# Half of an output projection as seven block products: layer 0's out-projection of a two-layer fp32 trunk on one Trainium2 core

## The chip, the cores and the metric

The kernel runs on one core of one Trainium2 chip. The metric is the device time of one execution in microseconds (us). Engines: PE is TensorE's matmul, PEld its weight load, DVE is VectorE, ACT is ScalarE, POOL is GpSimd, SP is SyncE, which here only issues transfers. An engine executes its instructions in the order in which they stand in the program, and waits on semaphores for what it needs.

## The reference

A causal trunk of two layers on a sequence of 512 tokens with model width 1024, everything in float32. Layer 0 is the one that matters here:

```python
xn = rms_norm(h, norm_mix[layer])
proj = jnp.einsum('bsd,de->bse', xn, w_in_even[i])
y_a = short_gated_conv(a_b, a_c, a_v, conv_a[i])        # 512 channels
y_b = multiscale_pool(z_b, w_pool[i], pool_scale[i])    # 512 channels
mix = jnp.concatenate([y_a, y_b], axis=-1)
h = h + jnp.einsum('bse,ed->bsd', mix, w_out_even[i])   # the output projection
hn = rms_norm(h, norm_ffn[layer])
h = h + gated_conv_ffn(hn, w_gate, w_up, conv_w, conv_b, w_down)
```

Then comes layer 1, with a gated mixer of another kind and an FFN of the same kind, and a last norm. The output projection of layer 0 multiplies the mix (512 tokens, 1024 channels: 512 of y_a, 512 of y_b) with a weight of 1024x1024.

## The kernel before, in words

**Number format.** Each operand of a matmul is split into a high part in fp32r and a low part, the rest; a product is three matmuls, high x high, high x low and low x high (`mm3`, L157 to L159). A weight gets its parts in one of two ways. `parts` (L149) copies the high part on ACT (L152) and subtracts on DVE (L153). `summed` (L138) copies the negative weight on ACT (L142), adds the weight onto it by a DMA on POOL's queue (L144), and copies the high part on ACT (L146). Tiles of weights are 128x1024; there are four "raw" slots for weights as they arrive (`fetch`, L130), and six each for high and low parts. A fetch waits until the slot's last reader is done.

**Layout.** The residual `h` lies as eight tiles of 128 channels x 512 tokens, and so does the mix: `mix[0..3]` of y_a, `mix[4..7]` of y_b. PSUM has seven banks for products and one for small things.

**Layer 0's mixer** (`mixer0`) makes groups of four banks: z, ac, av, then four pooled products pm (L527), then ab. The group ab ends with `b_done`, which multiplies the bank into a tile `cv` and splits it into high and low part.

**The output projection** (`project`, L303, called from `mixer0`, "oe" in the profile) has two halves of 512 output channels, `gi` = 0 and 1. A half is 4 column blocks x 8 k x 3 matmuls of 128x512, 96 in all. The first four k go through all four banks, the other four k ("tail") bank by bank, so that the banks end one after the other. For each one `done` adds the bank to `h[k]` on DVE (L315), and `norm.add` makes the scaled copy for the next product: ACT's high part hg (L202), DVE's low part (L203), ACT's square (L209, L212) and POOL's sum of squares (L213).

**The FFN of layer 0** (`Ffn`) comes next. Its first two channel tiles (f = 0) are a direct product of 512-column matmuls ("gu", `direct`, L645). Its weights come by `pair_weights` (L631, transfers L640). During gu the kernel makes sums of activation blocks (`block_sums`, L675 to L700; the first two of the four sets are split by adding DMAs on POOL, the others on ACT and DVE, L731 and L732), the norm's reciprocal root (`rstd_cols`, L246 to L256), and the weight sums of the next unit (`prepare`, L734 to L777). All later pairs of channel tiles are Strassen units (`products`, L785): seven products of 256-token blocks with 128-column weight blocks, by the helper `multiply` (L558 to L588), which lets products add up in the same half bank:

```python
BANK = {1: "a", 6: "a", 7: "a", 4: "a", 5: "e", 3: "e", 2: "b"}
```

What is in a bank is read out between products: by ACT's copy (L816) or by an add on DVE (L804). A product that goes on in a bank waits for that reader. In the unit f = 2 each product is 12 matmuls of 128x256; from f = 4 on high and low part of the moving block go together as one matmul of 512 columns (L571) and the low weights as one of 256.

**What sets the order.** The code is written without synchronisation: a scheduler lays the instructions of each engine in an order and inserts the waits, and the pools give out the slots. So an edit at one place can change the order of instructions on an engine some way beyond it. `tc.keep_in_program_order` and `behind` pin a few places by hand, none in the output projection.

Of the kernel before, what the change touches and what calls it, by code (L numbers as in the profile page):

```python
# [8 lines left out]
F32 = mybir.dt.float32  # L9
F32R = mybir.dt.float32r  # L10
BF16 = mybir.dt.bfloat16
AF = mybir.ActivationFunctionType
ALU = mybir.AluOpType
PSUM = bass.MemoryType.PSUM

P = 128
D = 1024
S = 512
# [13 lines left out]
def tile_trunk(ctx: ExitStack, tc: tile.TileContext, x, norm_mix, norm_ffn, final_norm,  # L32
# [3 lines left out]
    nc = tc.nc  # L36
    x = x[0]
# [92 lines left out]
    def fetch(src, a, b, name):  # L130
        raw = wp.tile([P, a, b], F32, tag="raw", bufs=4, name=f"raw_{name}")
        nc.sync.dma_start(raw, src)
        return raw, a, b, name
# [27 lines left out]
    def group(name, outs, ks, lhs, rhs, tail, on_done, before=None, at_end=None, begun=None):  # L161

        start, banks = begun or (0, {})
        head = max(0, len(ks) - tail)
        order = [(i, j) for i in range(start, head) for j in outs]
        order += [(i, j) for j in outs for i in range(head, len(ks))]
        at = start - 1  # L170
        for i, j in order:
            if i > at and before is not None:
                before(ks[i])
            at = max(at, i)
            if j not in banks:
                banks[j] = mm_bank(f"{name}_{j}")
            mm3(banks[j], lhs(ks[i], j), rhs(ks[i], j), i == 0, i == len(ks) - 1)
            if i == len(ks) - 1 and at_end is None:
                on_done(j, banks[j])
        if at_end is not None:  # L180
            at_end()
            for j in outs:
                on_done(j, banks[j])


    h = [cp.tile([P, S], F32, tag=f"h{k}", name=f"h{k}") for k in range(NK)]
    hg2 = [cp.tile([P, 2, S], F32R, name=f"hg{k}") for k in range(NK)]
    hg = [(t[:, 0], t[:, 1]) for t in hg2]

    def hg_k(k):  # L190
        return hg[k][0], hg[k][1]
# [71 lines left out]
    def split(pool, src, name, scale=1.0, tag="a", bufs=None):  # L263
        hi = pool.tile([P, S], F32R, tag=f"{tag}hi", bufs=bufs, name=f"{name}_hi")
        lo = pool.tile([P, S], F32R, tag=f"{tag}lo", bufs=bufs, name=f"{name}_lo")
        nc.scalar.activation(hi, src, AF.Copy, scale=scale)
        if isinstance(scale, float):
            nc.vector.tensor_tensor(lo, src, hi.bitcast(F32), ALU.subtract)
        else:
            nc.vector.scalar_tensor_tensor(lo, src, scale, hi.bitcast(F32),  # L270
                                           op0=ALU.mult, op1=ALU.subtract)
        return hi, lo
# [19 lines left out]
    def half_weights(name, w, ks, gi):  # L292

        chunks = {}
        for i in range(0, len(ks), 2):
            k0 = min(ks[i], ks[i + 1])
            hi, lo = weights(
                w[k0 * P : (k0 + 2) * P, gi * 512 : gi * 512 + 512]
                .rearrange("(k p) c -> p k c", p=P), 2, 512, f"{name}_{gi}_{k0}")
            chunks[k0], chunks[k0 + 1] = (hi, lo, 0), (hi, lo, 1)  # L300
        return chunks

    def project(name, w, acts, ks, norm, before=None, halves=(0, 1), tail=4):  # L303

        for gi in halves:
            chunks = half_weights(name, w, ks, gi)

            def lhs(k, j):
                hi, lo, n = chunks[k]
                cs = slice(j * P, (j + 1) * P)  # L310
                return hi[:, n, cs], lo[:, n, cs]

            def done(j, ps):
                k = gi * 4 + j
                nc.vector.tensor_tensor(h[k], ps, h[k], ALU.add)  # L315
                if norm is not None:
                    norm.add(k)

            group(f"{name}{gi}", range(4), ks, lhs, lambda k, j: acts[k], tail, done,
                  before if gi == 0 else None)  # L320


    prm0 = prm1 = None
# [5 lines left out]
    def in_parts(chunks, k, raw, after=(None, None)):  # L329
        hi, lo = parts(*raw, after=after)  # L330
        for i in range(raw[1]):
            chunks[k + i] = hi[:, i, :], lo[:, i, :]

    def in_group(name, w, c0, lhs_is_weight, on_done, tail, chunks=None, before=None,
                 after=(None, None), begun=None, after_later=None):
        if chunks is None:
            chunks = {}
            for k in range(0, NK, 2):
                in_parts(chunks, k, in_fetch(name, w, c0, k, 2),
                         after_later if k and after_later else after)  # L340

        def wt(k, j):
            cs = slice(j * P, (j + 1) * P)
            return chunks[k][0][:, cs], chunks[k][1][:, cs]

        def wt_wide(k, j):
            return chunks[k]

        def tokens(k, j):
            cs = slice(j * P, (j + 1) * P)  # L350
            return hg[k][0][:, cs], hg[k][1][:, cs]

        if lhs_is_weight:
            group(name, range(4), list(range(NK)), wt, lambda k, j: hg_k(k), tail, on_done, before,
                  begun=begun)
        else:
            group(name, range(4), list(range(NK)), tokens, wt_wide, tail, on_done, before)

    def mixer0():
        nonlocal prm0  # L360
        w = w_in_even[0]
        with tc.tile_pool(name="m0", bufs=1) as mp:
# [4 lines left out]
            norm = Norm("m0", lambda k: prm_mix["col"]("mix", k))  # L367
# [81 lines left out]
            mix = {}  # L449
# [3 lines left out]
            zs = {}  # L453
# [36 lines left out]
            prm0 = params0()  # L490
# [21 lines left out]
            cv = {}  # L512

            def v_done(j, ps):
                p = padded_tile()
                nc.vector.tensor_tensor(p[:, 2:], ps, ac[j], ALU.mult)
                if j % 2 == 0:
                    cv["pair"] = mp.tile([P, 2, S], F32, tag="four", bufs=5, name=f"cv{j}")
                t = cv["pair"][:, j % 2, :]
                conv3(t, p, *(prm0("ca", 4 * i + j) for i in range(3)))  # L520
                nc.gpsimd.tensor_tensor(t, t, rstd[0], ALU.mult)
                cv[j] = t

            in_group("av", w, 1024, True, v_done, 4)

            for g in range(4):
                ps = mm_bank(f"pm{g}")  # L527
                mm3(ps, (wpl_hi[:, g, :], wpl_lo[:, g, :]), pooled[g], True, True)
                mix[4 + g] = split(mp, ps, f"yb{g}", scale=prm0("psc", g), tag="mix", bufs=8)

            def b_done(j, ps):
                nc.vector.tensor_tensor(cv[j], ps, cv[j], ALU.mult)
# [2 lines left out]
            in_group("ab", w, 0, True, b_done, 4)  # L535

            nxt = Norm("f0", lambda k: prm0("ffn", k))
            project("oe", w_out_even[0], mix, [4, 5, 6, 7, 0, 1, 2, 3], nxt)
            return nxt

    STEPS = [(0, None, True), (2, (0, 2, 0), False), (4, (0, 2, 1), True)]
    for f in range(6, NF, 4):
        STEPS += [(f, (f - 4, f, 0), False), (f + 2, (f - 4, f, 1), f + 4 < NF)]
    HALF = S // 2
    NP = NK // 2
# [8 lines left out]
    def multiply(banks, name, product, left, right, both=None):  # L558

        at = BANK[product]
        first = at not in banks
        if first:
            banks[at] = mm_bank(f"{name}{at}")
        ps = banks[at][:, :HALF]
        if both is not None:
            for kp in range(NP):  # L570
                nc.tensor.matmul(banks[at], left(kp)[0], both(kp), start=first and kp == 0,  # L571
                                 stop=kp == NP - 1, skip_group_check=True)
            for kp in range(NP):
                last_matmul[0] = nc.tensor.matmul(ps, left(kp)[1], right(kp)[0], start=False,
                                                  stop=kp == NP - 1, skip_group_check=True)
            return banks[at]
        for kp in range(NP):
            (a_hi, a_lo), (b_hi, b_lo) = left(kp), right(kp)
            for l, r, end in ((a_hi, b_hi, False), (a_hi, b_lo, False),
                              (a_lo, b_hi, kp == NP - 1)):  # L580
                nc.tensor.matmul(ps, l, r, start=first, stop=end, skip_group_check=True)  # L581
                first = False
        return ps
# [8 lines left out]
    class Ffn:  # L592
# [109 lines left out]
        def moving(self, product, kp):  # L702

            if product in (1, 2, 3):
                k = kp if product == 1 else kp + NP
                c = slice(HALF, S) if product == 3 else slice(0, HALF)
                return hg[k][0][:, c], hg[k][1][:, c]
            if product in (6, 7):
                t = self.t23[kp][product - 6]
                return t[:, 0, :], t[:, 1, :]  # L710
            return tuple(t[:, {4: 0, 5: 1}[product], :] for t in self.t41[kp])
# [701 lines left out]
    n = mixer0()  # L1413
    n = ffn0(n)
    n = mixer1(n)
# [31 lines left out]
```

## Time and profile before

| | |
|---|---|
| median of 3 runs | 972.64 us (972.55 to 972.85) |
| the profiled execution | 972.66 us |
| its span in the trace | 970.9 us |
| granted PE clock, mean | 0.998 |
| first half of the output projection on PE | 100.62 to 122.38 us |
| its second half | 122.38 to 144.14 us |
| gu, the direct FFN unit | 144.14 to 167.32 us |
| f = 2, the first Strassen unit | 167.32 to 187.50 us |

Times in the trace count from the span's start. A line of the timeline gives start, duration, engine, source line and operation, then output <- inputs by the program's names with numbers left out (so `g_2a` is bank "a" of the gate in unit f = 2, and `wlo_g` any low part of a gate's weight), shape and, in brackets, how long the engine had been idle before and what released it. Line numbers are those of the kernel before; in the changed kernel the code behind `mixer0` stands 88 lines lower. Matmuls are pipelined, so their durations overlap and the distance between starts tells what one costs.

### The profile page before, as it was taken

The page shows a single profiled execution, that of the slowest core. Times are in us where ns is not written, and L with a number is a line of the kernel's source. Part 1 is how long each engine was busy: PE and PEld are TensorE (multiplying, and loading weights), DVE is VectorE, ACT ScalarE, POOL GpSimd, SP SyncE. Part 2 cuts the span into 40 slices and gives each one's busy share as a digit, 9 for nine tenths or more (in the row PEclk, how much of TensorE's full clock was granted, in tenths as well). Part 3 has the DMA queues.
Part 4 walks back from the last instruction along what each step waited for, and adds up shares of the span by engine and source line. Part 5 has one row for each costly group of instructions (what it writes and reads, how often), then busy time and mean ns, then how long its engine had stood idle before and what let it go on. Part 6 is the DMA issues. An engine that isn't in the chain of part 4 may idle for free.

```text
span 970.9 us, 13658 instructions
## 1 busy us (share of the span) xinstructions
PE 961.0 (99%) x4952; PEld 818.6 (84%) x4952; DVE 812.9 (84%) x1387; ACT 597.5 (62%) x895; POOL 152.0 (16%) x173
## 2 busy tenths in 40 slices
PE   9999999999999999999999999999999999999996
PEld 7888888988888888888888888889888888888885
DVE  6887458999898998998878675589998989889897
ACT  5523347765675665765586834587665666656775
POOL 3141023110111010110311001221111011100123
PEclk9999999999999999999999999999999999999999
DMA  7442225776777677774352333167767777668775
GB/s 252 149 137 86 87 88 111 178 180 161 195 175 168 157 174 195 168 176 135 128 153 87 109 109 108 51 136 182 185 142 196 195 174 174 159 162 200 195 154 139
DMA packets 92335, 148.33 MB, mean 153 GB/s; under 512 B 5124, under 2 KB 56300, under 8 KB 92268
## 3 DMA queue, kind: packets, MB, share of 16 engines
q1 hardware_dynamic: 76236, 98.69, 32.1%
q0 software_dynamic: 14256, 46.93, 26.8%
q10 hardware_dynamic: 1776, 1.84, 0.6%
q8 instruction: 39, 0.64, 0.3%
q14 instruction: 28, 0.23, 0.1%
HBM read 98.42 MB, written 2.10 MB: 104 GB/s over the span
## 4 chain that ended last, share of the span: by engine, by line
PE 94%; DVE 3%; DMA 1%; issue 1%; ACT 0%; POOLq 0%; DVEq 0%; POOL 0%
PE dn L158 3%; PE dn L159 3%; PE dn L157 3%; PE d L158 3%; PE d L157 3%; PE d L159 3%; PE vu_a L1026 2%; PE gu L157 2%; PE gu L159 2%; PE oo L159 2%; PE oo L157 2%; PE gu L158 2%; PE oe L159 1%; PE oe L158 1%; PE oo L158 1%; PE oe L157 1%
## 5 line engine op out<-in xcount | busy, mean ns | idle before, releaser
L144 POOL DMA_DIRECT2D wlo_g<-raw_g x20 | 17.2, 862 | 318.8 <-ACT wlo_g L142 118.3
L617 DVE SCALAR_TENSOR_TENSOR c<-rows,prm,c 128x512 f32<-128x512 f32 x88 | 65.3, 744 | 1.6 <-ACT c L615 1.4
L158 PE MATMUL dn<-wlo_dn,a_hi 128*128 128x512 f32 x144 | 56.2, 390 | 0.0
L158 PE MATMUL d<-a_lo,whi_d 128*128 128x512 f32 x144 | 56.2, 390 | 0.0
L159 PE MATMUL dn<-whi_dn,a_lo 128*128 128x512 f32 x144 | 56.2, 390 | 0.0
L159 PE MATMUL d<-a_hi,wlo_d 128*128 128x512 f32 x144 | 56.1, 390 | 0.0
L157 PE MATMUL d<-a_hi,whi_d 128*128 128x512 f32 x144 | 56.1, 390 | 0.0
L157 PE MATMUL dn<-whi_dn,a_hi 128*128 128x512 f32 x144 | 56.1, 390 | 0.0
L731 ACT ACTIVATE whi_a<-raw_g 128x512 fp32r<-128x512 f32 x20 | 12.6, 632 | 61.3 <-PE g_10e L571 9.0
L213 POOL TENSOR_TENSOR ssq_f<-ssq_f,sq_f 128x512 f32<-128x512 f32 x14 | 19.8, 1411 | 142.4 <-issue 102.0
L142 ACT ACTIVATE wlo_g<-raw_g 128x1024 fp32r<-128x1024 f32 x20 | 21.2, 1062 | 27.5 <-PE g_2e L581 8.8
L202 ACT ACTIVATE hg<-h,prm 128x512 fp32r<-128x512 f32 x24 | 17.3, 721 | 33.1 <-DVE h L315 33.1
L615 ACT ACTIVATE c<-rows,prm 128x512 f32<-128x512 f32 x44 | 31.4, 715 | 9.8 <-DVE rows L828 9.6
L625 ACT ACTIVATE s<-c,prm 128x512 f32<-128x512 f32 x44 | 31.4, 716 | 6.2 <-DVE c L617 6.1
L1201 DVE SCALAR_TENSOR_TENSOR y<-dn,small,y 128x512 f32<-128x512 f32 x40 | 28.0, 749 | 8.1 <-PE dn L159 8.1
L203 DVE SCALAR_TENSOR_TENSOR hg<-h,prm,hg 128x512 fp32r<-128x512 f32 x24 | 22.6, 944 | 11.9 <-ACT hg L202 11.9
L159 PEld LDWEIGHTS dn<-whi_dn,a_lo 128*128 128x128 f32 x144 | 27.0, 188 | 5.7
L159 PEld LDWEIGHTS d<-a_hi,wlo_d 128*128 128x128 f32 x144 | 27.0, 188 | 5.7
L153 DVE TENSOR_TENSOR wlo_dn<-raw_dn,whi_dn 128x1024 fp32r<-128x1024 f32 x18 | 22.0, 1224 | 11.7 <-ACT whi_dn L152 10.6
L157 PEld LDWEIGHTS d<-a_hi,whi_d 128*128 128x128 f32 x144 | 27.1, 188 | 5.4
L157 PEld LDWEIGHTS dn<-whi_dn,a_hi 128*128 128x128 f32 x144 | 27.1, 188 | 5.4
L158 PEld LDWEIGHTS dn<-wlo_dn,a_hi 128*128 128x128 f32 x144 | 27.0, 188 | 5.4
(1060 smaller groups left out, 3261.6 us busy)
## 6 DMA issues: line engine op xcount, KB each, us to landing
raw_g<-in_w_ffn_gate_dram SPq DMA_DIRECT2D x40, 512.0 KB, 3.8
raw_u<-in_w_ffn_up_dram SPq DMA_DIRECT2D x40, 512.0 KB, 4.3
raw_dn<-in_w_ffn_down_dram SPq DMA_DIRECT2D x22, 512.0 KB, 6.0
wlo_g<-raw_g POOLq DMA_DIRECT2D x20, 512.0 KB, 4.6
wlo_u<-raw_u POOLq DMA_DIRECT2D x20, 512.0 KB, 6.4
raw_d<-in_w_ffn_down_dram SPq DMA_DIRECT2D x18, 512.0 KB, 4.1
wlo_s12g<-s12g POOLq DMA_DIRECT2D x18, 512.0 KB, 6.3
wlo_s34g<-s34g POOLq DMA_DIRECT2D x18, 512.0 KB, 5.7
```

Source lines behind the costliest of these rows:

```text
L142: first = nc.scalar.activation(lo, raw, AF.Copy, scale=-1.0)
L153: behind(nc.vector.tensor_tensor(lo, raw, hi.bitcast(F32), ALU.subtract), after[0])
L157: nc.tensor.matmul(ps, lhs[0], rhs[0], start=start, stop=False)
L158: nc.tensor.matmul(ps, lhs[0], rhs[1], start=False, stop=False)
L159: nc.tensor.matmul(ps, lhs[1], rhs[0], start=False, stop=stop)
L203: nc.vector.scalar_tensor_tensor(hg[k][1], h[k], g, hg[k][0].bitcast(F32), op0=ALU.mult, op1=ALU.subtract)
L213: nc.gpsimd.tensor_tensor(self.ssq, self.ssq, sq, ALU.add)
L615: nc.scalar.activation(c, t[:, 0:S], AF.Copy, scale=prm("cf", ft))
L617: self.last_conv = nc.vector.scalar_tensor_tensor(c, t[:, i : S + i], prm("cf", i * NF + ft), c, op0=ALU.mult, op1=ALU.add)
L625: self.last_silu = nc.scalar.activation(s, c, AF.Silu, bias=self.prm("bf", ft))
L1026: nc.tensor.matmul(banks[at], lhs[l], rhs[r], start=first, stop=end, skip_group_check=True)
L1201: return nc.vector.scalar_tensor_tensor(dst, ps, ffn.cols[:, t : t + 1], dst, op0=ALU.mult, op1=ALU.add)
```

## The change

The second half of the output projection (output channels 512 to 1023) is computed by seven block products (Strassen's scheme in the same variant that the FFN uses) in place of the eight. Tokens are cut into two blocks of 256, the mix into y_a and y_b, and the weight's half into four blocks of 512 x 256. A product is then 4 k x 2 column blocks of 128 x 3 split terms, with 256 columns moving: 24 matmuls of 128x256, and all seven 168.

The block sums of activations are made on DVE during the first half, in place, on the float32 tiles of y_a (`cv`, read through `ya`) and of y_b, of which ACT now makes a float32 copy (`ybr`) beside the split parts. The sums get their own high and low parts: four of 128x512 in `hg4` to `hg7` (free at that time) and eight of 128x256 in slots of the mixer's pool (`t43`). Weight sums are made on DVE in the raw slots; weights of products 1, 2, 4 and 6 are split by `parts`, those of 5, 7 and 3 by `summed`. The order of the products is 1, 2, 6, 5, 7, 3, 4; after each product DVE adds its half bank to a half of `h[k]`, and `norm.add` follows product 3 for `h[4]` and `h[5]` and product 4 for `h[6]` and `h[7]`.

```diff
--- before.py
+++ after.py
@@ -516,17 +516,22 @@
                 nc.vector.tensor_tensor(p[:, 2:], ps, ac[j], ALU.mult)
                 if j % 2 == 0:
                     cv["pair"] = mp.tile([P, 2, S], F32, tag="four", bufs=5, name=f"cv{j}")
+                    ya.append(cv["pair"])
                 t = cv["pair"][:, j % 2, :]
                 conv3(t, p, *(prm0("ca", 4 * i + j) for i in range(3)))
                 nc.gpsimd.tensor_tensor(t, t, rstd[0], ALU.mult)
                 cv[j] = t
 
+            yb, ya = [], []
             in_group("av", w, 1024, True, v_done, 4)
 
             for g in range(4):
                 ps = mm_bank(f"pm{g}")
                 mm3(ps, (wpl_hi[:, g, :], wpl_lo[:, g, :]), pooled[g], True, True)
                 mix[4 + g] = split(mp, ps, f"yb{g}", scale=prm0("psc", g), tag="mix", bufs=8)
+                if g % 2 == 0:
+                    yb.append(mp.tile([P, 2, S], F32, tag="four", bufs=5, name=f"ybr{g}"))
+                nc.scalar.activation(yb[-1][:, g % 2, :], ps, AF.Copy, scale=prm0("psc", g))
 
             def b_done(j, ps):
                 nc.vector.tensor_tensor(cv[j], ps, cv[j], ALU.mult)
@@ -535,12 +540,95 @@
             in_group("ab", w, 0, True, b_done, 4)
 
             nxt = Norm("f0", lambda k: prm0("ffn", k))
-            project("oe", w_out_even[0], mix, [4, 5, 6, 7, 0, 1, 2, 3], nxt)
+            t43 = {}
+
+            def sums_of(k):
+                if k not in (1, 2):
+                    return
+                q = k - 1
+                block_sums_of(ya[q], yb[q])
+                for n in range(2):
+                    kp = 2 * q + n
+                    nc.scalar.activation(hg[4 + kp][0], ya[q][:, n, :], AF.Copy)
+                    nc.vector.tensor_tensor(hg[4 + kp][1], ya[q][:, n, :],
+                                            hg[4 + kp][0].bitcast(F32), ALU.subtract)
+                for i in range(2):
+                    for n in range(2):
+                        at = 4 * q + 2 * i + n
+                        tag, bufs = ("z", 4) if at < 4 else ("zs", 2) if at < 6 else ("pl", 2)
+                        t = mp.tile([P, 2, HALF], F32R, tag=tag, bufs=bufs, name=f"t43_{at}")
+                        src = yb[q][:, n, i * HALF : (i + 1) * HALF]
+                        nc.scalar.activation(t[:, 0], src, AF.Copy)
+                        nc.vector.tensor_tensor(t[:, 1], src, t[:, 0].bitcast(F32), ALU.subtract)
+                        t43[i, 2 * q + n] = t[:, 0], t[:, 1]
+
+            project("oe", w_out_even[0], mix, [4, 5, 6, 7, 0, 1, 2, 3], nxt, before=sums_of,
+                    halves=(0,))
+            project_blocks("oe1", w_out_even[0], mix,
+                           {6: lambda kp: tuple(x[:, :HALF] for x in hg[4 + kp]),
+                            5: lambda kp: tuple(x[:, HALF:] for x in hg[4 + kp]),
+                            4: lambda kp: t43[0, kp], 7: lambda kp: t43[1, kp]}, nxt)
             return nxt
 
 
 
 
+
+    def block_sums_of(y0, y1):
+
+        t3, t1, t2, t4 = y1[:, :, HALF:], y0[:, :, HALF:], y0[:, :, :HALF], y1[:, :, :HALF]
+        nc.vector.tensor_tensor(t3, t3, t1, ALU.subtract)
+        nc.vector.tensor_tensor(t1, t1, t2, ALU.subtract)
+        nc.vector.tensor_tensor(t2, t2, t3, ALU.add)
+        nc.vector.tensor_tensor(t4, t4, t2, ALU.subtract)
+
+    def project_blocks(name, w, acts, sums, norm):
+
+        raw = {}
+        for i, j in ((0, 0), (1, 0), (1, 1), (0, 1)):
+            raw[i, j] = fetch(w[i * 512 : (i + 1) * 512, 512 + j * HALF : 512 + (j + 1) * HALF]
+                              .rearrange("(k p) c -> p k c", p=P), 4, HALF, f"{name}_{i}{j}")
+        stat = {}
+
+        def put(product, how, at):
+            r, a, b, n = raw[at]
+            stat[product] = how(r, a, b, f"{n}_{product}")
+
+        def to(at, x, y, op):
+            nc.vector.tensor_tensor(raw[at][0], raw[x][0], raw[y][0], op)
+
+        a11, a12, a21, a22 = (0, 0), (1, 0), (0, 1), (1, 1)
+        put(1, parts, a11)
+        put(2, parts, a12)
+        put(4, parts, a22)
+        to(a22, a21, a22, ALU.add)
+        to(a21, a11, a21, ALU.subtract)
+        to(a11, a22, a11, ALU.subtract)
+        put(6, parts, a11)
+        to(a12, a12, a11, ALU.subtract)
+        put(5, summed, a22)
+        put(7, summed, a21)
+        put(3, summed, a12)
+
+        def moving(product, kp):
+            if product in (1, 2, 3):
+                c = slice(HALF, S) if product == 3 else slice(0, HALF)
+                return tuple(x[:, c] for x in acts[kp + (0 if product == 1 else NP)])
+            return sums[product](kp)
+
+        banks = ({}, {})
+        for product in (1, 2, 6, 5, 7, 3, 4):
+            for i in range(2):
+                hi, lo = stat[product]
+                c = slice(i * P, (i + 1) * P)
+                ps = multiply(banks[i], f"{name}_{i}", product,
+                              lambda kp: (hi[:, kp, c], lo[:, kp, c]),
+                              lambda kp: moving(product, kp))
+                k = 4 + i + 2 * (product in (5, 7, 4))
+                d = h[k][:, HALF:] if product in (6, 5, 7, 3) else h[k][:, :HALF]
+                nc.vector.tensor_tensor(d, ps, d, ALU.add)
+                if product in (3, 4):
+                    norm.add(k)
 
     STEPS = [(0, None, True), (2, (0, 2, 0), False), (4, (0, 2, 1), True)]
     for f in range(6, NF, 4):
```

## The prediction

> **What bounds the kernel now.** I read the page first, then the waits on PE, then the stages.
>
> ```profile
> span 970.9 us, 13658 instructions
> PE 961.0 (99%) x4952; PEld 818.6 (84%) x4952; DVE 812.9 (84%) x1387; ACT 597.5 (62%) x895; POOL 152.0 (16%) x173
> PE 94%; DVE 3%; DMA 1%; issue 1%; ACT 0%; POOLq 0%; DVEq 0%; POOL 0%
> ```
> ```profile
> PE clock L61 <- DVE idle L56: 1.3, 1, 1.3
> PE z L441 <- ACT hg L409: 0.3, 1, 0.3
> PE g_10a L571 <- DVE rows L804: 0.3, 1, 0.3
> PE u_10a L571 <- DVE kept L804: 0.2, 1, 0.2
> ```
>
> TensorE (PE) is busy for 99% of the span and is 94% of the chain that ended last; it waits 2.1 us in all, and 0.5 us of that falls behind the changed place. So the time is the sum of PE's instructions plus its stalls: whatever the edit takes off PE is won, unless a new wait gives it back. Now the stages, cut where PE begins another product (columns: stretch, its length, then the busy time of PE, PEld, DVE, ACT, POOL, the granted clock, DMA share, GB/s).
>
> ```profile
> 100.62:122.38 21.76, 21.76 (x97) 18.02 (x96) 10.23 (x12) 8.10 (x11) 1.71 (x2) 1.00 0.31 97
> 122.38:144.14 21.76, 21.76 (x97) 18.02 (x96) 11.44 (x12) 8.89 (x14) 5.56 (x5) 1.00 0.32 98
> 144.14:167.32 23.18, 23.18 (x109) 19.30 (x108) 20.72 (x42) 17.65 (x33) 9.25 (x9) 1.00 0.57 114
> 167.32:187.50 20.18, 20.18 (x170) 20.17 (x169) 19.87 (x33) 14.78 (x24) 2.59 (x3) 1.00 0.59 145
> ```
>
> They are the two halves of the output projection (oe), the direct FFN unit (gu, f = 0) and the first Strassen unit (f = 2). PE is full in each. VectorE (DVE) is half idle through oe, but full in the last stage (19.87 of 20.18) and nearly so in gu. The second row is what the change replaces.
>
> **The change part by part.** PE first. The row of oe's second half gives 96 matmuls of 128x512 in 21.76 us, 0.2267 us each, and all of it goes. Seven products of two 128-column blocks, four k and three split terms make 168 matmuls of 128x256. The only kernel code that already does this is the f = 2 unit:
>
> ```profile
> 167.32 0.40 PE L581 MATMUL g_2a<-hg,whi_a 128*128 128x256 f32 x2
> 168.76 0.40 PE L581 MATMUL u_2a<-hg,whi_a 128*128 128x256 f32 x2
> 177.40 0.40 PE L581 MATMUL g_2a<-t,whi_s34g 128*128 128x256 f32 x2
> 180.28 0.40 PE L581 MATMUL u_2a<-t,whi_s34u 128*128 128x256 f32 x2
> ```
>
> One block of 12 takes 168.76 - 167.32 = 1.44 us, 0.12 each (busy spans overlap, starts count). Fourteen blocks make 20.16 us. **PE is 21.76 - 20.16 = 1.60 us shorter**: 1/8 fewer columns would be 2.72, but a 256-column matmul costs 0.53 of a 512-column one. The stage row says why: PEld, the weight loads, is busy 20.17 of 20.18 us, so at 256 columns the loads are the limit.
>
> The Trainium skill speaks against the edit here: TensorE: Matmul & The Clock Gate, section "Back-to-back issue gap", gives a sustained gap of about 81 ns at N=128 and 131 ns at N=512. Taken between, about 98 ns at 256 (my estimate), 168 would take 16.5 us and 96 of the long ones 12.6, a loss of 3.9 us. This case's rows, 120 against 226.7 ns, disagree with both figures and have the other sign, so I keep the rows.
>
> Next DVE and ACT in the first half. New on DVE: eight block sums (two lists of four; 128x2x256), four low parts of 128x512, eight of 128x256, four weight sums of 128x1024; evacuation becomes 14 adds of 128x256 for four of 128x512. Nearest rows:
>
> ```profile
> 112.62 1.23 DVE L153 TENSOR_TENSOR wlo_oe<-raw_oe,whi_oe 128x1024 fp32r<-128x1024 f32 x1 [4.21 <-ACT whi_oe L152]
> 114.42 0.69 DVE L315 TENSOR_TENSOR h<-oe,h 128x512 f32<-128x512 f32 x1 [0.58 <-PE oe L159]
> 179.62 0.42 DVE L804 TENSOR_TENSOR rows<-g_2a,rows 128x256 f32<-128x256 f32 x1
> 115.15 0.72 ACT L202 ACTIVATE hg<-h,prm 128x512 fp32r<-128x512 f32 x1 [2.56 <-DVE h L315]
> 175.00 0.38 ACT L816 COPY rows<-g_2a 128x256 f32<-128x256 f32 x1
> ```
>
> DVE gets 12 x 0.69 + 8 x 0.42 + 4 x 1.23 = 16.6 us, and the evacuations 14 x 0.42 - 4 x 0.69 = 3.1 us more. The idle time of DVE in the two halves is 11.5 + 10.3 = 21.8 us, so PE hides this. ACT gets four yb copies (2.9 us) in the stage before, then four copies at 0.72, eight at about 0.4 and ten weight copies of 128x1024 where four go (6 x 1.06): 12.4 us, and its idle time in the two halves is 13.7 + 12.9. I cost all that at nothing. If the cover were gone, a late operand of products 1 to 4 would show as a PE wait at its product.
>
> Third, weights of products 5, 7 and 3. Each is summed: an ACT copy, then a DMA on POOL's queue that adds into it. And the "raw" slots (four) have one order: u_0's fetch waits for product 5's adding DMA to land, g's second half for product 7's. Their low parts stand on DVE, in the built order, ahead of evacuations that free PE's banks: wlo_u ahead of product 5's adds, which product 3 needs; the second wlo_g ahead of product 7's, which product 4 needs. Rows for the transfers (median us from issue to landing last) and the splits:
>
> ```profile
> wlo_g<-raw_g POOLq DMA_DIRECT2D x20, 512.0 KB, 4.6
> wlo_u<-raw_u POOLq DMA_DIRECT2D x20, 512.0 KB, 6.4
> raw_u<-in_w_ffn_up_dram SPq DMA_DIRECT2D x40, 512.0 KB, 4.3
> 106.08 1.06 ACT L152 ACTIVATE whi_oe<-raw_oe 128x1024 fp32r<-128x1024 f32 x1 [3.08 <-PE oe L158]
> ```
>
> With the products 1, 2, 6, 5, 7, 3, 4 at 122.38 + 2.88 each, product 3 starts at 136.78 and 4 at 139.66. ACT reaches product 5's first copy at about 121.1 (its slot is freed by PE then) and has both done by 123.2; the adding DMA issues there and lands at 128.2 with 5.0 (between the two rows; 127.8 to 129.6). The fetch then lands at 131.5 to 132.5, ACT's copy and DVE's split (1.06 + 1.23) end at 133.8 to 134.9, and product 5's two adds finish by 135.2: 1.6 us early. With 6.4 and 4.3 in a row it would be 129.6 + 4.3 + 0.4 (second issue) + 2.3 + 0.8 = 137.4, or 0.6 us late. The same sum for product 7 leaves 2.0 us. I take no wait; the ends are 0 and about 1.1 us.
>
> Fourth, the start of the FFN. PE arrives 1.6 us early at gu and at f = 2, but the work there does not move with it. All of h4 to h7 is complete only with products 3 and 4, so low parts and block sums crowd behind the end of oe. In the built order ACT's copy t_3 stands ahead of the norm's square root and waits for POOL's adding DMAs of the t's, so the reciprocal comes at 155.0, no earlier than now; and the two splits wlo_a, at the start of gu before, stand behind it. DVE in gu had 23.18 - 20.72 = 2.5 us to spare. The rows:
>
> ```profile
> 146.50 0.68 DVE L732 TENSOR_TENSOR wlo_a<-raw_u,whi_a 128x512 fp32r<-128x512 f32 x1
> 155.13 0.17 DVE L247 RECIPROCAL rc_f0c<-sd_f0c 128x4 f32<-128x4 f32 x1
> 160.70 1.23 DVE L732 TENSOR_TENSOR wlo_s12g<-s12g,whi_s12g 128x1024 fp32r<-128x1024 f32 x1
> 165.55 1.30 DVE L664 TENSOR_TENSOR rows<-gu,rstd_f 128x512 f32<-128x512 f32 x2 [0.56 <-PE gu L159]
> 167.59 1.23 DVE L732 TENSOR_TENSOR wlo_s12u<-s12u,whi_s12u 128x1024 fp32r<-128x1024 f32 x1 [0.74 <-PE gu L159]
> 170.06 2.07 DVE L617 SCALAR_TENSOR_TENSOR c<-rows,prm,c 128x512 f32<-128x512 f32 x3
> 172.21 1.28 ACT L625 ACT_TABLE_LOAD   x1 [0.62 <-DVE c L617]
> 173.51 1.34 ACT L625 ACTIVATE s<-c,prm 128x512 f32<-128x512 f32 x2
> ```
>
> DVE waited 0.56 and 0.74 us for gu here, so it was ahead of PE by 1.3 us; then it is never idle until 188.7. Behind the reciprocal now come two splits more (2 x 0.6, a start every 0.08 us less than the duration) and about 1.0 us of t_2's parts that came ahead of it; less the 1.3 us of waits and 0.1 of the reciprocal, the third c ends some 0.8 us later than 170.06 + 2.07 = 172.1, though PE is 1.6 us earlier. ACT waits for that c, loads its table (1.28), does two silus (1.34) and only then the copy of g_2a's bank (175.00 + 0.38), on which product 7 of f = 2 waits (177.40, with 2.0 us to spare). So the copy is done at 175.38 + 0.8 = 176.2, and PE is there at 177.40 - 1.60 = 175.8. **A stall of 0.3 to 0.5 us.** The next tight place is in f = 4:
>
> ```profile
> 202.82 0.86 PE L571 MATMUL g_4a<-t,whi_s34g 128*128 128x512 f32 x3
> 201.93 0.42 DVE L804 TENSOR_TENSOR rows<-g_4a,rows 128x256 f32<-128x256 f32 x1
> 189.28 0.75 DVE L617 SCALAR_TENSOR_TENSOR c<-rows,prm,c 128x512 f32<-128x512 f32 x1 [0.57 <-ACT c L615]
> 200.79 1.23 DVE L153 TENSOR_TENSOR wlo_d<-raw_d,whi_d 128x1024 fp32r<-128x1024 f32 x1 [0.43 <-ACT whi_d L152]
> ```
>
> PE takes the bank at 202.82, 0.47 us after DVE's add (201.93 + 0.42), and DVE can catch up at most the two gaps of 0.57 and 0.43, of which ACT keeps a part. A DVE that is 0.5 us late against the old clock allows PE to be early by about 0.5 to 1.0. I take 0.8 as PE's gain that is left here; behind f = 4 the program is the old one with PE full, so the shift lasts to the end.
>
> **Sum.** The profiled execution took 972.66 us (span 970.9 and 1.8 around it), 0.02 over the median of 972.64, so nothing is scaled. 972.66 - 1.60 + 0.8 = **971.9 us**.
>
> **The rivals.**
> 1. *PE's whole gain arrives*, 972.66 - 1.60 = 971.1. For it: DVE's 1.3 us of waiting for gu; the 2.0 us at product 7. Against: the crowd behind products 3 and 4. The sharpest limit is the 0.47 us of f = 4.
> 2. *DVE's queue at the FFN's start takes it all*, 972.4 to 973.0: the chain c, table load, silu, copy comes 1 us later than I reckon, and the stall at product 7 is 1.3 us or more. DVE would then show no wait for gu.
> 3. *Slower: the queue of transfers into PE's banks.* The place is product 3's first matmul, or 4's. Both transfers in a row 1.6 us longer than reckoned, as under contention (DMA share in these halves is 0.3), and PE waits on wlo_u's split. Price by the 6.4 and 4.3 rows: 0.6 to 1.1 at product 3, as much again at 4, then the 0.8 to 1.6 of the FFN's start on top, since a late PE does not make DVE early: 973.0 to 975.5.
> 4. *The edit does not do what it says*: short matmuls cost PE more than half of long ones here, by more than f = 2 shows. From 21.76/168 = 0.130 us each they save nothing, 972.7. All rows of f = 2 stand at 0.120, so this has 0.02 and lies within rival 2's range. By the gaps of the Trainium skill (TensorE: Matmul & The Clock Gate, section "Back-to-back issue gap") it would be 972.66 + 3.9 = 976.6 and slower; the same rows speak against that.
>
> **How the numbers follow.** Forecast (971.3 to 972.4) 0.52; rival 1 0.14; rival 2 0.12 and rival 4 0.02; rival 3 0.20, about half of it above 974.6. A measurement of this kernel tells about 0.2%, 1.9 us, from no change; PE's gain is 1.6 plus at most the 0.5 of old waits, so faster by more is nearly shut out: 0.03. Slower by more needs 3.5 us of new waits: 0.12. The rest, 0.85, is within. The range 971.0 to 973.8 leaves out 0.02 below and about 0.15 above.
>
> **What would show it.** PE's first gu matmul at 142.5 in place of 144.14, and 1.44 us between blocks of oe, show the PE sum; waits on PE at products 3 or 4 (banks e and a) against DVE adds show rival 3. A PE wait at g_2a's product 7 on ACT's copy of about 0.4 us, and one at g_4a on rows of about the same, show the fourth step; neither, and rival 1 has it. What would make me wrong altogether is a wait in front of product 1 or 2 (operands not ready at 122.4), which I took to be hidden.

## The result, and the profile after

The changed kernel takes 977.03 us (median of 5 runs, 976.79 to 978.84) against 972.70 of the kernel before in the same comparison; the ratio is 1.0049, 95% interval 1.0035 to 1.0063. It is 4.3 us slower, outside the range 971.0 to 973.8. Four executions in the later comparisons, two of them of the kernel before, took 3.9 to 5.2 ms and are left out of the medians; one was the profiled run of e3 (below), whose profile therefore comes from e9. The page of its profile, with the lines that answer to those of before:

```profile
span 975.3 us, 13869 instructions
...
PE 961.7 (99%) x5024; PEld 822.9 (84%) x5024; DVE 831.1 (85%) x1421; ACT 610.8 (63%) x917; POOL 154.3 (16%) x176
...
PE 91%; DVE 6%; DMA 1%; issue 1%; ACT 1%; DVEq 0%; POOLq 0%; POOL 0%; SPq 0%; ACTq 0%
```

PE is busy no less than before (961.7 against 961.0 us, although the matmuls should have become 1.6 us cheaper; a stretch at a lower clock, below, accounts for 1.55). Its share of the chain that ended last falls from 94 to 91%, and DVE's rises from 3 to 6%. The waits on PE, longest first:

```profile
PE oe_0e L669 <- DVE h L629: 3.3, 1, 3.3
PE clock L61 <- DVE idle L56: 1.3, 1, 1.3
PE g_10a L659 <- DVE rows L892: 0.7, 1, 0.7
```

One new wait of 3.3 us stands at product 3's first matmul (bank e, L669), for DVE's add L629, which reads product 5 out of that bank. Around it, PE and DVE in order of time:

```profile
123.15 0.28 PE L669 MATMUL oe_0a<-ya_hi,whi_oe 128*128 128x256 f32 x1
...
124.58 0.28 PE L669 MATMUL oe_1a<-ya_hi,whi_oe 128*128 128x256 f32 x1
...
137.42 0.28 PE L669 MATMUL oe_1a<-t,wlo_oe 128*128 128x256 f32 x1
140.96 0.35 PE L669 MATMUL oe_0e<-yb_hi,whi_oe 128*128 128x256 f32 x1 [3.26 <-DVE h L629]
...
148.27 0.40 PE L157 MATMUL gu<-hg,whi_g 128*128 128x512 f32 x1
```
```profile
139.25 1.23 DVE L153 TENSOR_TENSOR wlo_u<-raw_u,whi_u 128x1024 fp32r<-128x1024 f32 x1 [6.11 <-ACT whi_u L152]
140.40 0.42 DVE L629 TENSOR_TENSOR h<-oe_0e,h 128x256 f32<-128x256 f32 x1
```

Product 5's two adds could have run when its matmuls ended, at about 133.4 and 134.8. They stand behind wlo_u, and DVE idles 6.11 us in front of wlo_u, whose raw weights are not there. Then the granted clock (the eighth column; the last two are DMA share and GB/s), in slices of 2 us:

```profile
100.62:122.40 21.78, 21.78 (x98) 18.04 (x97) 21.71 (x33) 12.09 (x23) 1.56 (x1) 1.00 0.00 1
...
136.00:138.00 2.00, 1.70 (x15) 1.49 (x13) 0.00 (x0) 0.00 (x0) 0.00 (x0) 1.00 1.04 300
138.00:140.00 2.00, 0.00 (x0) 0.00 (x0) 0.75 (x1) 1.43 (x2) 0.00 (x0) 1.00 1.02 309
140.00:142.00 2.00, 1.04 (x9) 1.07 (x10) 2.00 (x4) 1.59 (x2) 0.00 (x0) 1.00 1.04 322
142.00:144.00 2.00, 2.00 (x13) 2.00 (x12) 2.00 (x5) 0.15 (x1) 0.00 (x0) 0.59 0.85 255
144.00:146.00 2.00, 2.00 (x13) 2.00 (x12) 1.07 (x4) 1.45 (x3) 0.17 (x1) 0.56 0.85 248
146.00:148.00 2.00, 2.00 (x19) 2.00 (x18) 1.38 (x3) 1.54 (x3) 1.92 (x2) 1.00 0.80 263
```

Behind the wait PE is granted 0.59 and 0.56 for two slices and does 13 matmuls in each where a full slice holds 19. The first row shows two things more: DVE is full in the first half of oe (21.71 of 21.78 us), and no weights move there (DMA share 0.00), so that they all move in the second half (share about 1.0).

**The account up to gu.** Against before, gu begins 148.27 - 144.14 = 4.13 us late:
- +0.77: product 1 begins at 123.15 in place of 122.38. The lag is there at z in the first 7 us (0.71 of it), ahead of any changed instruction, and two kernels below that share before's program up to there show 0.82 and 0.33. It belongs to the execution.
- +3.42: PE's stop, from 137.54 (0.12 behind the last start) to 140.96.
- +1.55: the clock. From 140.96 the last four blocks should take 4 x 1.44 = 5.76 us, and take 7.31.
- -1.61: the rest, and what the cheaper matmuls were to save (1.60).

From gu to the end the distance stays within 0.5 us of 4.15.

### The profile page after: what moved, and what is told of

It is laid out like the page before. It is cut to its first block, busy times and chain, and to the rows that moved or that the text cites. A ratio compares the mean times of both kernels' runs of the same rounds, so it can differ in the third digit from the quotient of the medians.

```text
span 975.3 us, 13869 instructions
## 1 busy us (share of the span) xinstructions
PE 961.7 (99%) x5024; PEld 822.9 (84%) x5024; DVE 831.1 (85%) x1421; ACT 610.8 (63%) x917; POOL 154.3 (16%) x176
## 4 chain that ended last, share of the span: by engine, by line
PE 91%; DVE 6%; DMA 1%; issue 1%; ACT 1%; DVEq 0%; POOLq 0%; POOL 0%; SPq 0%; ACTq 0%
PE dn L158 3%; PE dn L159 3%; PE dn L157 3%; PE d L158 3%; PE d L159 3%; PE d L157 3%; PE vu_a L1114 2%; PE gu L157 2%; PE gu L159 1%; PE oo L159 1%; PE gu L158 1%; PE oo L157 1%; PE oo L158 1%; PE u_2a L669 1%; PE g_2a L669 1%; PE u_4a L669 1%
## 5 line engine op out<-in xcount | busy, mean ns | idle before, releaser
L266 ACT ACTIVATE a_hi<-s 128x512 fp32r<-128x512 f32 x40 | 24.9, 627 | 11.4 <-PE d L159 7.7
L158 PEld LDWEIGHTS d<-a_lo,whi_d 128*128 128x128 f32 x144 | 27.0, 188 | 5.4
```

The source lines that it names most:

```text
L158: nc.tensor.matmul(ps, lhs[0], rhs[1], start=False, stop=False)
```

## The experiments

The kernels change the changed kernel unless said otherwise; ratios are to the kernel before. Theory A: three things in a row make the wait. The fetch of u may start only when product 5's adding transfer has landed; it then shares the transfer engines with two adding transfers more; and DVE's fixed order puts its split ahead of the add for which PE waits. Rivals: PE would wait there for something else, or DVE, full in the first half, is late with everything.

**Splits behind the adds** (e1). `behind` (the helper that pins an instruction after another on its engine) puts two splits on DVE after product 7's adds. Here and below the cuts show the lines that matter; `read_out` holds the last add of each product:

```diff
-                ch[key, half] = parts(raw, 4, 2 * P, name)
+                behind_ = read_out.get({("u", 0): 7, ("g", 1): 7}.get((key, half)))
+                ch[key, half] = parts(raw, 4, 2 * P, name,
+                                      after=(behind_ if self.layer == 0 else None, None))
```

> The one edit: on DVE the two low parts wlo_u (first half) and wlo_g (second half) of the next FFN's weights stand behind product 7's adds instead of ahead of product 5's and 7's. All transfers stay. Theory A (the wait is in-order DVE work: product 5's adds stood behind a split whose fetch lands at 138.1): the wait of 3.3 us at oe_0e goes, the fetch of u still lands some 8 us after its issue, the granted clock stays at 1.0 and PE reaches gu at 142.5 + 0.7 = 143.3; the time is 977.03 - 3.4 - 1.55 = 972.1, give or take 0.5. Rival B (PE would wait there anyway, for product 3's weights, whose adding transfer landed at 137.7, or for DVE, full in the first half): a wait of more than 1 us stays at products 3 or 4, and the time is above 974.

Measured 974.36 us, ratio 1.0018 (1.0009 to 1.0027). The fetch is as late as before (u's copy on ACT at 137.96), the wait at product 3 is gone, the clock stays at 1.0 and gu begins at 142.94, 20.15 us behind product 1: the whole 1.60 is there. But the time is 2.3 us over what A gave. The splits, now behind, delay the last adds, and PE pays first at the norm (L230), then in f = 4 and f = 10:

```profile
...
PE ssc_f L230 <- POOL ssq_f L213: 1.0, 1, 1.0
PE g_10a L661 <- DVE rows L896: 0.8, 1, 0.8
...
PE g_4a L661 <- DVE rows L896: 0.3, 1, 0.3
```

So the order on DVE turned the late fetch into a wait of PE's, as A has it, but the lateness does not vanish with the order.

**Fewer adding transfers**: none (e2), product 5's alone (e4), all but product 5's (e3, and e9 for its profile). The edits are in `project_blocks`; e2 has all three, e4 the last two, e3 and e9 the first:

```diff
-        put(5, summed, a22)
+        put(5, parts, a22)
-        put(7, summed, a21)
-        put(3, summed, a12)
+        put(7, parts, a21)
+        put(3, parts, a12)
```

> Products 5, 7 and 3 get their low weights from DVE (three splits of 128x1024, 1.22 each) in place of ACT's negative copy and an adding DMA; DVE's order is otherwise that of the change. Theory A with its first half (the fetch took 8.5 us because three adding transfers shared the transfer engines with it): u's fetch lands about 4 us after its issue, no wait at product 3, clock 1.0, time about 972. Rival C (DVE is full from 100.6 to 124 and any more work there comes late): three splits more, 3.4 us, make product 5's or 7's weights late, with waits of 1 to 3 us at products 6 to 7 and a time of 974 to 977.

> Products 7 and 3 get their low weights from DVE, product 5 keeps its adding DMA, for whose landing u's fetch still waits. If the crowd of adding transfers is what made the fetch long: it is issued at about 129.5 and lands at about 133.5, the wait at product 3 goes, clock 1.0, time about 972. If the order of the slots (a fetch that may start only when the adding transfer has landed) were enough by itself: a wait of 2 us or more stays at product 3, time 975 or more.

> Only product 5 gets its low weights from DVE; products 7 and 3 keep their adding DMAs. Then u's fetch waits for no adding transfer to land (its slot is free after product 5's split, at about 126), but it goes out while product 7's and 3's adding transfers run. If the landing of product 5's adding DMA is what held the chain up: the wait at product 3 (3.3 us) goes, time about 972.5. If the crowd of adding transfers is, wherever the fetch starts: g's second half, whose slot waits for product 7's adding DMA, lands late, and a wait of 1 us or more stays at product 4, time 974 or more.

> The kernel with only product 5 by DVE's split once more, for a profile: its runs gave 973.97, so the wait at product 3 cannot be whole. If adding transfers slow whatever fetch runs beside them: PE waits 0.5 to 1.5 us at product 4 (g's second half comes late and stands on DVE ahead of product 7's adds) and not at product 3. If the chain held on product 5's landing alone: no wait in the projection, and the loss of 1.3 us lies at the FFN's start.

Measured: e2 973.46, ratio 1.0008 (0.9999 to 1.0017); e4 972.45, 0.9999 (0.9990 to 1.0008); e3 973.94, 1.0013 (1.0005 to 1.0022). None has the 3.3 us. The issue of the adding transfers on POOL's queue (products 5, 7, 3 in the change, 7 and 3 in e9; e4 has product 5's alone, at 124.50), the issue of u's fetch on SP (two in the row) and the ACT copy that waits for its landing, in the change, in e4 and in e9:

```profile
124.33 1.04 POOL L144 DMA_DIRECT2D wlo_oe<-raw_oe  x1
128.21 0.87 POOL L144 DMA_DIRECT2D wlo_oe<-raw_oe  x1
129.56 1.70 SPq L728 DMA_DIRECT2D raw_u<-in_w_ffn_up_dram  x2
129.96 0.85 POOL L144 DMA_DIRECT2D wlo_oe<-raw_oe  x1 [0.89 <-ACT wlo_oe L142]
138.16 1.06 ACT L152 ACTIVATE whi_u<-raw_u 128x1024 fp32r<-128x1024 f32 x1 [6.61 <-DMA raw_u<-in_w_ffn_up_dram]
```
```profile
129.79 1.03 SPq L728 DMA_DIRECT2D raw_u<-in_w_ffn_up_dram  x2
133.41 1.06 ACT L152 ACTIVATE whi_u<-raw_u 128x1024 fp32r<-128x1024 f32 x1 [3.19 <-DMA raw_u<-in_w_ffn_up_dram]
```
```profile
124.75 1.05 POOL L144 DMA_DIRECT2D wlo_oe<-raw_oe  x1 [0.70 <-DVE hg L203]
126.36 1.74 SPq L728 DMA_DIRECT2D raw_u<-in_w_ffn_up_dram  x2
128.69 0.88 POOL L144 DMA_DIRECT2D wlo_oe<-raw_oe  x1 [0.19 <-issue]
133.34 1.06 ACT L152 ACTIVATE whi_u<-raw_u 128x1024 fp32r<-128x1024 f32 x1 [3.07 <-DMA raw_u<-in_w_ffn_up_dram]
```

In e4 the fetch starts as late as in the change and takes 3.6 us; beside the adding transfers of products 7 and 3 it takes 8.6 (8.7 in e1, which has the same transfers), and 7.0 in e9. So those two transfers cost it 3 to 5 us, in one profile of each kernel. But e9, where it starts 3.2 us sooner and is slow as well, has no wait in the projection either (gu 20.15 us behind product 1): the wait needed the late start and the crowd together, and, by e1, DVE's order. Two of my expectations missed: the wait at product 4 in e3 did not come (the loss lies at the FFN's start, where PE in e9 waits 1.1 us at product 7 of f = 2 for ACT), and rival C has a part in e2, where product 6 waits 0.9 us for DVE's add and the time is 1.5 us over the 972 expected.

**Working through the wait** (e5: 31 extra matmuls; e6: 12; the number is `NBUSY`).

```diff
+            if product == 3:
+                spare = aux_bank("spare")
+                w7, x7 = stat[7][0], moving(7, 3)[0]
+                for n in range(NBUSY):
+                    inorder(nc.tensor.matmul(spare[:, :HALF], w7[:, 3, :P], x7, start=n == 0,
+                                             stop=n == NBUSY - 1))
```

> 31 extra matmuls of 128x256 with product 7's weights into a spare bank, between products 7 and 3, so that PE works through the 3.4 us in which the change waits; nothing else is altered, and nothing reads the bank. If the fall of the granted clock from 142.3 to 145.7 follows from PE having been idle: the clock stays at 1.0 and the time falls by 1.4 to 1.7 us, to about 975.5, although PE has more to do. If the fall comes from something else (the transfers, the short matmuls): the time stays at 977.0 or rises.

> 12 extra matmuls instead of 31 between products 7 and 3, so that PE is idle for about 2.0 us of the 3.4. If the granted clock falls only after an idle time that nearly fills one of its windows (the run with 3.4 us idle fell to 0.56 for 3.4 us): no fall, and the time is 977.03 - 1.55 = 975.5 or the 976.2 of the run with 31. If any idle time of PE brings the fall: clock below 0.8 for some us behind the wait, time near 977.

Measured: e5 976.16, ratio 1.0037 (1.0023 to 1.0051), 0.9 us faster than the change with 3.7 us more of matmuls (its slowest run took 976.68, the fastest of the change 976.79; 1.4 to 1.7 had been expected). Its clock at the place, then that of e6 with the wait that is left there, then that of e10 (below), where PE waits 1.3 us for DVE in f = 6:

```profile
142.00:144.00 2.00, 2.00 (x19) 2.00 (x18) 2.00 (x4) 0.56 (x1) 0.00 (x0) 1.00 0.82 257
144.00:146.00 2.00, 2.00 (x19) 2.00 (x18) 1.54 (x5) 1.50 (x3) 0.11 (x1) 1.00 0.83 250
```
```profile
142.00:144.00 2.00, 2.00 (x11) 2.00 (x11) 2.00 (x5) 0.00 (x0) 0.00 (x0) 0.50 0.80 248
144.00:146.00 2.00, 2.00 (x15) 2.00 (x15) 0.81 (x3) 1.43 (x3) 0.41 (x1) 0.73 0.78 246
```
```profile
PE oe_0e L676 <- DVE h L636: 1.8, 1, 1.8
```
```profile
226.00:228.00 2.00, 0.90 (x4) 0.80 (x5) 1.87 (x6) 1.32 (x2) 0.00 (x0) 1.00 0.27 47
228.00:230.00 2.00, 2.00 (x15) 1.78 (x13) 1.98 (x5) 1.58 (x3) 0.00 (x0) 1.00 1.05 373
```

PE kept busy keeps its clock: the 1.55 us are the price of the stop. In e5 gu begins 23.88 us behind product 1, against 25.12 in the change: 1.24 less, the 1.55 without the 0.3 by which 31 matmuls overrun the wait. In e6 PE was idle for 1.8 us only, and the fall came just the same (gu 25.11 us behind product 1, as in the change; 977.88 us, ratio 1.0056, 1.0042 to 1.0069; why the time is over the change's was not followed up). The expectation that a short stop goes free was wrong for 1.8 us; the waits of 0.9 in e2, 1.0 in e1, 1.1 in e9 and 1.3 in e10 left the clock at 1.00. Each is one stop in one profile: the length at which the fall begins was not measured more closely, nor whether it depends on the moment at which the stop comes.

**Where the 1.60 us went in e4.** Shift of PE's start against before at four places, each less the shift at product 1: gu -1.61, product 7 of f = 2 -1.37, u's product 2 in f = 4 (204.29 against 204.22) -0.87, and behind f = 10 (d at 299.86) -0.57. So 0.74 us were lost by f = 4 and 0.30 more by the end of f = 10. The -0.57 is no gain that is left: e8 (below), which has no seven products, comes to 0.04 - 0.82 = -0.78 there by the same reckoning. The rows of e4 in f = 2 show the queue that the prediction named, ACT's silu and copy and the matmul behind it:

```profile
175.05 1.34 ACT L713 ACTIVATE s<-c,prm 128x512 f32<-128x512 f32 x2
...
176.55 0.37 ACT L904 COPY rows<-g_2a 128x256 f32<-128x256 f32 x1
```
```profile
176.97 0.39 PE L669 MATMUL g_2a<-t,whi_s34g 128*128 128x256 f32 x1
```

The copy ends at 176.92 and PE begins at 176.97.

**One copy ahead on ACT** (e7 is e4 with it, e8 the kernel before with it). In e4 DVE idles 3.1 us in gu for t_2, which ACT makes behind the splits of t_0. Now ACT makes t_0, t_1 and t_2 first (`scale_in` is the copy that stood in `block_sums`; the splits of t_0 on ACT are pinned behind t_2's copy):

```diff
+                if self.layer == 0:
+                    for kp in range(3):
+                        self.scaled[kp] = self.scale_in(kp)
                 for kp in range(NP):
                     self.block_sums(kp)
```

> As the run with products 7 and 3 by DVE's splits (972.45, where PE came out of the projection 1.6 us early and lost 0.7 of it by f = 4 and 0.3 more at f = 10), and ACT makes the scaled copy t_2 ahead of the splits of t_0, which stood before it while DVE was idle for 3.1 us waiting for t_2. If the loss behind the projection comes from DVE's queue at the FFN's start: DVE's idle 3.1 us is used, the stalls at product 7 of f = 2 and f = 4 go, and the time is 0.5 to 1.0 us lower, 971.5 to 972.0. If ACT's own queue (table load, silu, copy) sets it: 972.4 as before.

> The kernel before with that one move of t_2's copy and nothing else. It tells whether the move is worth something by itself: PE waits 2.1 us in all there, 0.5 behind this place, so at most 0.5 us: 972.2 to 972.8. Its profile also has the same first 100 us of program as the kernel before: where PE's first products start tells whether the 0.4 to 0.9 us by which the changed kernels' profiles start later come with the change or from execution to execution.

Measured: e7 972.62, 0.9997 (0.9988 to 1.0006); e8 972.72, 1.0002 (0.9994 to 1.0011). In e7 the stall at product 7 of f = 2 is gone (0.02 us in place of 0.24), and the time is the same, where 0.5 to 1.0 us less had been expected: what PE keeps is lost at f = 10 instead.

```profile
PE clock L61 <- DVE idle L56: 1.3, 1, 1.3
PE g_10a L659 <- DVE rows L900: 0.9, 1, 0.9
```
```profile
263.91 0.69 DVE L848 TENSOR_TENSOR s12g<-raw_g,raw_g 128x512 f32<-128x512 f32 x1 [2.08 <-DMA raw_g<-in_w_ffn_gate_dram]
```

DVE waits there 2.08 us for a fetch (1.51 in the kernel before). e8 shows the same limit from the other side: its PE is 0.82 us later than before's from product 1 to f = 8, and 0.04 later behind unit f = 10. And e7's PE is 1.04 us earlier than e8's up to f = 8, and 0.13 earlier behind f = 10: what PE gains ahead of that unit, the unit takes.

**g's halves first in f = 10** (e10 is e7 with it, e11 is e8 with it, e12 is e10 once more).

```diff
-            raws = ffn_weights(layer, f, [(key, half) for half in range(2) for key in "gu"])
+            order = [(key, half) for half in range(2) for key in "gu"]
+            if layer == 0 and f == 10:
+                order = [("g", 0), ("g", 1), ("u", 0), ("u", 1)]
+            raws = ffn_weights(layer, f, order)
```

> The run with t_2's copy ahead, and in unit f = 10 of layer 0 both halves of g's weight are fetched before u's. In the runs so far PE waits 0.9 to 1.0 us at product 7 of g in f = 10 for DVE, and DVE had waited 2.1 to 2.3 us for g's second half. If that fetch is the next limit behind the one for DVE at the FFN's start: DVE waits 0.5 to 1.5 us less, PE's wait falls by as much, and 0.5 to 0.9 us of the projection's gain arrive: 971.7 to 972.1. If DVE's other work sets it: 972.6 as before.

> Control: the kernel before with the same two moves (t_2's copy ahead, g's halves first in f = 10). PE waits 0.3 and 0.2 us in f = 10 there, so at most 0.5 us can come: 972.2 to 972.7. What the run with seven products is faster than this one is the worth of the seven products themselves, at most 1.6 us.

> The fastest kernel so far once more, for a profile: its ten other runs gave 970.9 to 971.5, but the profiled one 973.45, with a wait of 1.3 us at g's product in f = 6. If that wait belongs to the kernel: it is there again. If it was of that execution alone: PE comes out of f = 4 some 1.0 us ahead of the kernel before, counted from the same start, waits less than 0.5 us in f = 10, and the time is 971.0 to 971.6.

Measured: e10 971.34, ratio 0.9988 (0.9979 to 0.9997); e11 972.27, 0.9996 (0.9987 to 1.0005). With seven products and the three moves the kernel is 1.1 us faster than before, and 0.9 faster than its control, of 1.6 at most; ten of e10's eleven runs took 970.92 to 971.54, and the fastest of the control 971.53. e12's profile was of a run of 972.31, which missed the 971.0 to 971.6 expected; DVE's wait is 1.58 us there, PE's in f = 10 is 0.4 (0.9 in e7), and the wait of 1.3 us at f = 6 in e10's profile (a run of 973.45) is not in it, so it does not come in every execution. No profile is of one of those ten runs, so where along the program their gain is kept is not shown.

## Why the prediction was wrong

1. *PE is 1.60 us shorter*: right. Blocks start 1.43 to 1.44 us apart, and in e4, without a wait, gu begins 143.47 - 123.32 = 20.15 us behind product 1 (20.16 predicted). Rival 4 is out, and with it the loss worked out from the Trainium skill's gaps (TensorE: Matmul & The Clock Gate, section "Back-to-back issue gap").
2. *The sums are hidden in the first half*: right, but barely. 11.5 us of the new work fell in the first half (DVE is busy for 21.71 us there, against 10.23), where DVE is now full; product 1 followed without a wait. I had held the work against the idle time of both halves.
3. *The transfers: "I take no wait; the ends are 0 and about 1.1 us"*: this is the step that failed. The start was well placed (u's fetch at 129.56; 128.2 predicted, and 0.77 of the difference is the late execution). The duration was not: 8.6 us where I had put 3.3 (for which I gave no row) to 4.3. My other durations, and the upper end, came from medians of transfers in calmer places; I did not add up what would run at once. The raw slots were held through the first half (in the kernel before, the four fetches of g and u go out there, at 101.77 to 113.87), so three adding transfers and four fetches met within 15 us, at a DMA share of 1.0. The 0.3 that I quoted for these halves was the share of the old program. Mechanism and place were those of rival 3; its size was 3.4 us, not 0.6 to 1.1.
4. *What a stop of PE costs beyond its length*: not in the sum at all. It was 1.55 us (e5). The Trainium skill has it (TensorE: Matmul & The Clock Gate, section "What's actually happening": after an idle window of about 3.4 us the array falls to half its clock until it has been busy for such a window). The trace agrees in the depth (0.50 to 0.59) and in the length of the fall (3.4 us, from 142.35 to 145.74). It differs in the idle time: 3.3 us, and even 1.8, were enough here, less than the window that the Trainium skill asks for, and the measurement decides.
5. *The start of the FFN gives back 0.8 us*: right in size and place where it can be seen (e4: 0.74 by f = 4, product 7 of f = 2 on ACT's copy). In the changed kernel it costs nothing, for PE arrives 4 us late and DVE has the time to catch up; rival 3 was wrong to add it on top. And the forecast overlooked the next limit, f = 10, which takes what is left (e7's lead of 1.04 us over e8 becomes 0.13).

Without the two adding transfers that crowd the fetch (e4) the time is 972.45, 0.55 above the forecast of 971.9: no difference from the kernel before that the runs can tell (0.9990 to 1.0008), as the prediction had held likeliest for the change. So the change loses in the projection by the wait and the clock, 3.42 + 1.55 us, and neither was in the sum.

## What to carry to other kernels

Where a change holds buffers through a stage, count the transfers that must then run in the next one, and price each by the rate that they share, not by its median elsewhere. Look on every in-order engine for an instruction that waits on a transfer ahead of one that frees a bank for the bounding engine. And a gain on the bounding engine arrives only if the engine behind it is not already the limit at some later place: find that place, by its smallest slack, before counting the gain.

## What had not been expected of the hardware

An idle time of PE of 1.8 us brought 3.4 us at half the clock, the same as one of 3.3 us, while stops of 0.9 to 1.3 us brought none; filling the 3.4 us with useless matmuls made the kernel 0.9 us faster. A fetch of 512 KB took 3.6 us with no adding transfer beside it and 7.0 to 8.7 us beside two.
